# Both ends of a one-core encoder-block kernel rearranged: the last residual on TensorE, the final root on ScalarE, blocks 2 and 3 of the last down half in steps, the second v weights converted by VectorE

## The chip, the core and the metric

The kernel runs on one core of a Trainium2 chip. A core has a matrix engine (TensorE, PE in the profile; its weight loads are PEld), three engines for elementwise work (VectorE, DVE; ScalarE, ACT; GpSimd, POOL), an engine that mostly issues transfers (SyncE, SP) and 16 DMA engines. Each engine works through a queue of its own in order and waits on semaphores that others set. The metric is the device time of one execution in microseconds (us); before the change the median of three executions is 701.1 (700.32 to 701.42). The profile comes from one more execution, which took 700.69 us.

## What is computed

One layer of an encoder over 512 positions of width 1024 in float32, then a last RMSNorm:

```
h = rms_norm(x, norm_mix_g)
proj = h @ w_in                      # conv B, C, in | q | k | v | forget logits | gates
y_conv = (cb * dwconv3(cc * cin)) @ w_out_conv
y_attn = forgetting_attention(q, k, v, log_f) @ w_out_attn
x = x + (g_conv * y_conv + g_attn * y_attn) @ w_o
h = rms_norm(x, norm_ffn_g)
a, b = split(dwconv3(h @ w_up))
x = x + (silu(a) * b) @ w_down       # 2816 hidden
return rms_norm(x, norm_f_g)
```

The start of the program (the projection to v) and its end (the product with `w_down`, the residual and the last norm) are what the change touches.

## The kernel before

Everything is kept transposed: 128 features on the partitions, 512 positions in the free dimension, so x is eight blocks (m = 0 to 7) of 128 x 512. Every product is made of three matrix passes: each operand is split into a high part in the fast float32r format and a low part that holds the rest, and high x high, low x high and high x low are added in PSUM. The splitting of weights is done while TensorE works on the block before: `split` has ScalarE convert the raw block to its high part (line 244) and VectorE subtract it for the low part (line 248). The raw blocks come from memory by a stream of transfers on SyncE's queue, five buffers deep; the high and low parts have two buffers each, so the split of a block waits until TensorE has left the block before the last one.

**The start.** The first eight blocks of the stream are the v weights (v0 to v7, 128 x 520). v0 is brought in two pieces (ScalarE's queue and SyncE's) and its high part is made by VectorE; from v1 on all come by SyncE and ScalarE makes the high parts. For each block x is split too: ScalarE makes `xgh`, VectorE `xgl`. TensorE's products for block kb need `xgh` and `wh_v` first, then `wl_v`, then `xgl`.

**The product with w_down.** The 22 hidden blocks are taken in two halves (`PHASES`: 0 to 11, 12 to 21), each after its part of the up product. Most of it runs as a Strassen-like scheme, function `down`: two output blocks (2i and 2i+1), two hidden blocks (a pair q) and the two halves of the positions make a 2 x 2 x 2 product, done with seven products of 128 x 128 x 256 instead of eight (`PROD`). A step holds two such pairs; its weights are sums of weight blocks, which transfers with accumulation have built in memory long before (`group`, `tick`), and come in two pieces, `P` (three products for each pair, 768 columns) and `F` (four, 1024 columns). `STEPS` lists which (i, q) a step takes: in the last half, before the change, five steps for the blocks i = 2 and i = 0. When a pair of blocks has had its last step, `combine` adds the seven sums into x: one copy on ScalarE and six operations on VectorE (z1, a1, u3 twice, a2, a3, a4), followed by the square of each block for the last norm (`final_square`: a square and a scaling on ScalarE, an add into `ssq3` on VectorE). These follow-ups are put on a list, `later`, and emitted by `run_later` beside the splits, or at the latest by `flush`.

The blocks m = 2, 3, 6 and 7 of the last half are plain (`PLAIN`): ten hidden blocks, two halves of the positions, three passes. m = 2 and 3 come first (`pd`); m = 6 and 7 come last and in halves of the positions: the first half of both (`pdA`, bank halves), then m = 6 second half (`pdB6`) and m = 7 second half (`pdB7`).

**The end.** For each half t of the positions, `fin_sum` adds the residual (VectorE), squares and scales (ScalarE); `fin_col` adds the squares of m = 6 to `ssq3` and has TensorE sum over the partitions (`pc`); `rstd_col` makes the inverse root: VectorE forms mean + eps (`ms`), GpSimd raises it to -0.5 (`rc`). `rstd_bc` lets TensorE spread it over the partitions (`pb`); `fin_out` copies `pb` to SBUF on ScalarE (`rs`) for GpSimd's share, multiplies the eight blocks in five groups on VectorE (four) and GpSimd (one), and sends each to memory. The column sum of the first half stands after five of the ten hidden blocks of `pdB6`, its `pb` after the rest of them. Nine products without use (`warm_on`) keep TensorE at work around the last `pc`.

The order on the engines is set by a list scheduler within what `keep` fixes (all matrix products and the marked operations stay in program order).

Of the kernel before, what the change touches and what calls it, by code (L numbers as in the profile page):

```python
# [13 lines left out]
P = 128  # L14
# [34 lines left out]
    (((2, 6), (2, 7)), ((2, 8), (2, 9)), ((0, 6), (0, 7)), ((0, 8), (2, 10)), ((0, 9), (0, 10))),  # L49
# [5 lines left out]
PLAIN = [(m, k) for m in (2, 3, 6, 7) for k in range(*PHASES[1])]  # L55
PCUTS = (0, 8, 16, 20, 28, 32, 40)
# [3 lines left out]
def block_kernel(ctx, tc, xT, vecs, wv, win, wmix, wo, wup, wst, wdp, outT):  # L60
# [57 lines left out]
    groups += [list(range(n, min(n + 2, NFF))) for n in range(0, NFF, 2)]  # L118
    todo = []

    def group(i):

        ns = groups[i]
        t = dsp.tile([P, len(ns), D], F32, tag=f"sum{i}", name=f"sum{i}")
        for k, n in enumerate(ns):
            sums[n] = t[:, k, :]
        w = wst[ns[0] : ns[-1] + 1].rearrange("n p c -> p n c")
        w, f = ((lambda a, b, z=z: z[:, :, a * P : b * P]) for z in (w, t))
# [24 lines left out]
    def double(n):  # L153
        return [(f"P{n}", wst[n, :, : 6 * P], 6 * P), (f"F{n}", sums[n], D)]
# [34 lines left out]
    def load(upto):  # L189
        for k in range(len(raws), min(upto, len(stream) - 1) + 1):  # L190
            nm, src, ncol = stream[k]
            if held[0] == NRAW:
                return
            held[0] += 1
            raw = wp.tile([P, D], F32, tag="raw", name=f"raw_{nm}", bufs=NRAW)
            if k == 0:

                keep(nc.scalar.dma_start(raw[:, :VW], src[:, :VW]))
                keep(nc.sync.dma_start(raw[:, VW:ncol], src[:, VW:]))
            else:  # L200
                keep(nc.sync.dma_start(raw[:, :ncol], src))
            raws.append(raw[:, :ncol])
# [20 lines left out]
    def split(hl=None):  # L223
# [16 lines left out]
        if k == 0:  # L240
            for cs in (slice(0, VW), slice(VW, S + H)):
                keep(nc.vector.tensor_copy(hi[:, cs], raw[:, cs]))
        else:
            ins = nc.scalar.activation(hi, raw, AF.Copy)  # L244
            order["hi"] = ins.ins
            if k < KB:
                keep(ins)
# [6 lines left out]
        run_later(k, {"u": 1.7, "P": 1.6, "F": 0.75}.get(nm[0], 3.5))  # L254
# [46 lines left out]
    ex = cp.tile([P, NT], F32, tag="ex", name="ex")  # L301
    nc.gpsimd.memset(ex, -0.5)
# [5 lines left out]
    def place_of(f, s_):  # L308
        c = 2 * (f % 3 if f < 6 else 3) + s_
        return slice(c * P, (c + 1) * P)  # L310
# [19 lines left out]
    def rstd_col(sums, n, bc, name):  # L330
# [9 lines left out]
        ms = cp.tile([P, NT], F32, tag="ms", name=f"ms_{name}", bufs=2)  # L340
        nc.vector.tensor_scalar(ms[:, :n], pc[:, :n], 1.0 / D, EPS, op0=ALU.mult, op1=ALU.add)
# [742 lines left out]
    def down(ph, n0):  # L1084

        sets = ({0: X, 1: Y, 3: X, 2: Y}, {0: X, 2: Y})[ph]
        todo, wants = [], {}
        for n, d in enumerate(STEPS[ph]):
            for kind in "PF":
                prods = []  # L1090
                for s_, (i, q) in enumerate(d):
                    for f, g, b, h in PROD:
                        if (f < 3) == (kind == "P"):
                            wants.setdefault(f"{kind}{n0 + n}", []).append(("q", q))
                            prods.append((place_of(f, s_), i, place(ph, q) + g, b, h))
                todo.append((f"{kind}{n0 + n}", prods))
# [64 lines left out]
    for m, b in ((2, 4), (3, 2)):  # L1161
        flush((b,))
        p = bank(b, f"pd{m}")
        for k in kall:
            for t in range(2):
                plain(m, t, (k,), p[:, th[t]], t == 0, t == 1)
        nc.vector.tensor_add(x1[:, m, :], p, x1[:, m, :])
        later.append((0, 0.8, (), lambda m=m: final_square(m)))

    m6 = KB - 2  # L1170
    fetch(3)
    wx = fp.tile([P, 6, 2 * P], F32R, tag="gr", name="wx").rearrange("p a b -> p (a b)")
    fetch(4, [wx[:, a : a + 4 * P] for a in (80, 752)])
    fetch(5)
    flush()
    pdA, pdB6, pdB7 = bank(3, "pdA"), bank(5, "pdB6"), bank(0, "pdB7")
    pd = ((pdA[:, th[0]], pdA[:, th[1]]), (pdB6[:, th[0]], pdB7[:, th[0]]))

    def plain7(m, t, ks):
        plain(m6 + m, t, ks, pd[t][m], m == 0 or t == 1, m == 1 or t == 1)  # L1180

    def fin_sum(t, m):

        y = x1[:, m6 + m, halves[t]]
        nc.vector.tensor_add(y, pd[t][m], y)
        sq = fp.tile([P, S], F32, tag="fu", name=f"sq3_{m}{t}", bufs=3)[:, : S // 2]
        nc.scalar.activation(sq, y, AF.Square)
        nc.scalar.activation(y, y, AF.Copy, scale=col(GF + m6 + m))
        return sq

    def fin_col(t, sqs):
        s_ = ssq3[:, halves[t]]
        nc.vector.tensor_add(s_, s_, sqs[0])
        return rstd_col([s_, sqs[1]], 2, 6 + t, f"n3{t}")

    def fin_out(t, rc):
# [15 lines left out]
    warm_to = bank(2, "warm_to")[:, : 2 * P]  # L1212
# [20 lines left out]
def _layout(i):  # L1233
# [47 lines left out]
    for d in STEPS[0] + STEPS[1]:  # L1281
        wst.append(np.concatenate([wdn[2 * i + m, :, 2 * q + k] for m, k in order for i, q in d], axis=1))
# [44 lines left out]
```

## Time and profile before

| | |
|---|---|
| median of three executions | 701.1 us |
| profiled execution, whole | 700.69 us |
| its span (first to last instruction) | 698.9 us |
| busy: TensorE / VectorE / ScalarE / GpSimd | 690.2 / 498.3 / 341.8 / 156.4 us |
| bytes read / written | 112.20 / 32.51 MB |

"Busy" is the sum of an engine's instruction times; the rows of the timeline give start, duration, engine, line, operation and tiles (output <- inputs). In brackets stands how long the engine was idle before, and who ended it. In the chain of waits each row is a start and the time that the chain spends there. Two rows of the profile may overlap on one engine, since instructions are pipelined: the step from start to start is shorter than the duration.

### The profile page before, as it was taken

The page shows a single profiled execution, that of the slowest core. Times are in us where ns is not written, and L with a number is a line of the kernel's source. Part 1 is how long each engine was busy: PE and PEld are TensorE (multiplying, and loading weights), DVE is VectorE, ACT ScalarE, POOL GpSimd, SP SyncE. Part 2 cuts the span into 40 slices and gives each one's busy share as a digit, 9 for nine tenths or more (in the row PEclk, how much of TensorE's full clock was granted, in tenths as well). Part 3 has the DMA queues.
Part 4 walks back from the last instruction along what each step waited for, and adds up shares of the span by engine and source line. Part 5 has one row for each costly group of instructions (what it writes and reads, how often), then busy time and mean ns, then how long its engine had stood idle before and what let it go on. Part 6 is the DMA issues. An engine that isn't in the chain of part 4 may idle for free.

```text
span 698.9 us, 14573 instructions
## 1 busy us (share of the span) xinstructions
PE 690.2 (99%) x6005; PEld 688.1 (98%) x6005; DVE 498.3 (71%) x797; ACT 341.8 (49%) x541; POOL 156.4 (22%) x176
## 2 busy tenths in 40 slices
PE   9999999999999999999999999999999999999996
PEld 8999999999999999999999999999999999999995
DVE  6677777786687787754377777778774677877853
ACT  6665656655664433543345443455443345444542
POOL 5125645434011001035321212230000211100002
PEclk9999999999999999999999999999999999999998
DMA  8627877467379777658556637577675433224503
GB/s 308 201 74 209 200 158 200 118 163 179 92 176 268 232 212 214 225 183 207 140 133 197 170 106 199 141 171 206 191 222 177 116 118 92 84 84 133 177 1 121
DMA packets 51538, 115.31 MB, mean 165 GB/s; under 512 B 4720, under 2 KB 22256, under 8 KB 51472
## 3 DMA queue, kind: packets, MB, share of 16 engines
q1 hardware_dynamic: 36880, 93.73, 41.4%
q0 software_dynamic: 13328, 19.44, 17.5%
q10 hardware_dynamic: 1264, 1.22, 0.5%
q8 instruction: 47, 0.77, 0.4%
q14 instruction: 19, 0.16, 0.1%
HBM read 112.20 MB, written 32.51 MB: 207 GB/s over the span
## 4 chain that ended last, share of the span: by engine, by line
PE 92%; DVE 2%; ACT 2%; issue 1%; DMA 1%; ACTq 0%; SPq 0%; POOL 0%; DVEq 0%
PE p_up L277 26%; PE p_in L277 14%; PE dn L295 12%; PE p_up L295 8%; PE gs L295 8%; PE p_wo L277 6%; PE yc L295 3%; PE ya L277 3%; PE pd L277 2%; PE o L659 2%; PE pa L478 2%; PE pb L480 1%; PE tp L644 1%; PE pdB L277 1%; PE pdA L277 1%
## 5 line engine op out<-in xcount | busy, mean ns | idle before, releaser
L277 PE MATMUL p_up<-x1h,wh_up 128*128 128x256 f32 x536 | 104.5, 276 | 0.0
L277 PE MATMUL p_up<-x1l,wh_up 128*128 128x256 f32 x536 | 104.4, 276 | 0.0
L277 PE MATMUL p_up<-x1h,wl_up 128*128 128x256 f32 x536 | 104.3, 276 | 0.0
L244 ACT ACTIVATE wh_up<-raw_up 128x1024 fp32r<-128x1024 f32 x44 | 46.7, 1061 | 89.2 <-PE p_up L277 75.7
L277 PEld LDWEIGHTS p_up<-x1h,wh_up 128*128 128x128 f32 x536 | 80.8, 188 | 0.0
L277 PEld LDWEIGHTS p_up<-x1l,wh_up 128*128 128x128 f32 x536 | 80.7, 188 | 0.0
L277 PEld LDWEIGHTS p_up<-x1h,wl_up 128*128 128x128 f32 x536 | 80.6, 188 | 0.0
L134 POOL DMA_DIRECT2D sum<-in_wst_dram x45 | 47.1, 1122 | 116.4 <-DMA sum<-sum 88.8
L248 DVE TENSOR_TENSOR wl_up<-raw_up,wh_up 128x1024 fp32r<-128x1024 f32 x44 | 53.8, 1223 | 20.8 <-ACT wh_up L244 20.8
L244 ACT ACTIVATE wh_F<-raw_F 128x1024 fp32r<-128x1024 f32 x29 | 30.8, 1063 | 54.6 <-PE ya L277 25.9
L277 PE MATMUL p_in<-xgh,wh_in 128*128 128x256 f32 x288 | 56.8, 279 | 0.0
L277 PE MATMUL p_in<-xgh,wl_in 128*128 128x256 f32 x288 | 56.6, 278 | 0.1
L277 PE MATMUL p_in<-xgl,wh_in 128*128 128x256 f32 x288 | 56.5, 277 | 0.0
L976 DVE TENSOR_TENSOR fz<-p_up,rb_n 128x512 f32<-128x512 f32 x44 | 30.3, 690 | 31.3 <-PE p_up L277 31.3
L248 DVE TENSOR_TENSOR wl_F<-raw_F,wh_F 128x1024 fp32r<-128x1024 f32 x29 | 35.5, 1223 | 17.5 <-ACT wh_F L244 17.5
L277 PEld LDWEIGHTS p_in<-xgh,wh_in 128*128 128x128 f32 x288 | 44.7, 188 | 0.7
L989 POOL TENSOR_TENSOR ge<-fu,fu 128x512 f32<-128x512 f32 x11 | 17.1, 1551 | 120.3 <-DVE fu L573 107.5
L277 PEld LDWEIGHTS p_in<-xgh,wl_in 128*128 128x128 f32 x288 | 43.6, 188 | 0.3 <-DVE wl_in L248 0.3
L277 PEld LDWEIGHTS p_in<-xgl,wh_in 128*128 128x128 f32 x288 | 43.6, 188 | 0.0
L295 PE MATMUL p_up<-x1h,wh_up 128*128 128x256 f32 x168 | 40.3, 277 | 0.0
L295 PE MATMUL p_up<-x1l,wh_up 128*128 128x256 f32 x168 | 40.2, 276 | 0.0
L244 ACT ACTIVATE wh_P<-raw_P 128x768 fp32r<-128x768 f32 x29 | 24.4, 842 | 26.1 <-PE dn L295 14.1
(307 smaller groups left out, 2044.5 us busy)
## 6 DMA issues: line engine op xcount, KB each, us to landing
raw_up<-in_wup_dram SPq DMA_DIRECT2D x44, 512.0 KB, 4.3
raw_F<-sum SPq DMA_DIRECT2D x29, 512.0 KB, 4.6
raw_in<-in_win_dram SPq DMA_DIRECT2D x24, 512.0 KB, 4.5
raw_P<-in_wst_dram SPq DMA_DIRECT2D x29, 384.0 KB, 3.5
sum<-in_wst_dram POOLq DMA_DIRECT2D x29, 256.0 KB, 5.6
sum<-in_wst_dram SPq DMA_DIRECT2D x14, 512.0 KB, 5.6
sum<-in_wst_dram POOLq DMA_DIRECT2D x14, 512.0 KB, 7.3
sum<-sum SPq DMA_DIRECT2D x28, 256.0 KB, 5.9
```

Of the source, the lines that this page charges most:

```text
L134: return lambda: keep(nc.gpsimd.dma_start(dst, src, accum_op=ALU.add))
L244: ins = nc.scalar.activation(hi, raw, AF.Copy)
L248: ins = nc.vector.tensor_sub(lo, raw, hi.bitcast(F32))
L277: keep(nc.tensor.matmul(out[:, cs], w, x[:, cs], start=start and i == 0 and c == 0, stop=stop and i == 2 and c == len(cut) - 1,))
L295: keep(nc.tensor.matmul(out, wl if x == 1 else wh, xl if x == 2 else xh, start=opens and bk not in seen, stop=closes and bk not in left,))
L478: keep(nc.tensor.matmul(pa[t][:, :VW], xt, w[:, :VW], start=start, stop=stop))
L480: keep(nc.tensor.matmul(pb[t], xt, w[:, VW:], start=start and t % 2 == 0, stop=stop and t % 2 == 1))
L644: keep(nc.tensor.transpose(tp[:, ks], pt[:, ks], ident))
L659: keep(nc.tensor.matmul(o[:, os_], vv[:, kb, pr, e, :], x[:, kb, cs], start=e == 0 and kb == 0 and i == 0, stop=e == 1 and kb == nk - 1 an ...
L976: nc.vector.tensor_mul(z, p, rb2)
L989: keep(nc.gpsimd.tensor_mul(ge, a.rearrange(halves_of, h=2), b.rearrange(halves_of, h=2)))
```

## The change

- The blocks 2 and 3 of the last down half (i = 1) are no longer plain but take steps: (1,6)/(1,7), (1,8)/(1,9) and a last step with the single pair (1,10). A step with one pair has half the columns; its group of sums stands alone. In step 15 the two pairs change places. `PLAIN` holds m = 6 and 7 only.
- The second half of the residual of m = 7 is split into high and low parts and added by TensorE, as two products with the identity into `pdB7`; the last square and scaling read PSUM directly.
- For the two final column sums, ScalarE takes the root of mean + eps (Sqrt) and VectorE the reciprocal, instead of VectorE and GpSimd's power.
- In `fin_out`, the first group's multiplication comes ahead of ScalarE's copy of `pb`.
- The second v block comes on ScalarE's queue, and VectorE makes its high part.
- Splits of the `dp` blocks carry no follow-up work with them (`"d": 0`).

```
-    (((2, 6), (2, 7)), ((2, 8), (2, 9)), ((0, 6), (0, 7)), ((0, 8), (2, 10)), ((0, 9), (0, 10))),
+    (
+        ((2, 6), (2, 7)), ((2, 8), (2, 9)), ((0, 6), (0, 7)), ((2, 10), (0, 8)), ((0, 9), (0, 10)),
+        ((1, 6), (1, 7)), ((1, 8), (1, 9)), ((1, 10),),
+    ),
-PLAIN = [(m, k) for m in (2, 3, 6, 7) for k in range(*PHASES[1])]
-PCUTS = (0, 8, 16, 20, 28, 32, 40)
+PLAIN = [(m, k) for m in (6, 7) for k in range(*PHASES[1])]
+PCUTS = (0, 4, 12, 20)
...
-                keep(nc.sync.dma_start(raw[:, :ncol], src))
+                keep((nc.scalar if k == 1 else nc.sync).dma_start(raw[:, :ncol], src))
...
-        if k == 0:
-            for cs in (slice(0, VW), slice(VW, S + H)):
+        if k < 2:
+            for cs in (slice(0, VW), slice(VW, S + H)) if k == 0 else (slice(0, S + H),):
                 keep(nc.vector.tensor_copy(hi[:, cs], raw[:, cs]))
...
-        run_later(k, {"u": 1.7, "P": 1.6, "F": 0.75}.get(nm[0], 3.5))
+        run_later(k, {"u": 1.7, "P": 1.6, "F": 0.75, "d": 0}.get(nm[0], 3.5))
...
+        if n == 2:
+            nc.scalar.activation(ms[:, :n], pc[:, :n], AF.Sqrt, bias=eps, scale=1.0 / D)
+            rc = cp.tile([P, NT], F32, tag="rc", name=f"rc_{name}", bufs=2)
+            nc.vector.reciprocal(rc[:, :n], ms[:, :n])
+            return rc
...
-    for m, b in ((2, 4), (3, 2)):
...
+    idr = gh[:, 40, :P]
+    nc.scalar.activation(idr, ident, AF.Copy)
+    xlast = (gh[:, 41, :], gl[:, 41, :])
+    y7 = x1[:, KB - 1, halves[1]]
+    nc.scalar.activation(xlast[0], y7, AF.Copy)
+    nc.vector.tensor_sub(xlast[1], y7, xlast[0].bitcast(F32))
...
+        if m + t == 2:
+            for i, x in enumerate(xlast):
+                keep(nc.tensor.matmul(pd[t][m], idr, x, start=i == 0, stop=False))
...
-        nc.vector.tensor_add(y, pd[t][m], y)
+        r = y
+        if m + t == 2:
+            r = pd[t][m]
+        else:
+            nc.vector.tensor_add(y, pd[t][m], y)
...
-        nc.scalar.activation(rs, pb, AF.Copy)
...
-            eng.tensor_mul(y, y, r.unsqueeze(1).to_broadcast([P, b - a, S // 2]))
+            keep(eng.tensor_mul(y, y, r.unsqueeze(1).to_broadcast([P, b - a, S // 2])))
+            if g == 0:
+                keep(nc.scalar.activation(rs, pb, AF.Copy))
```

The queues show what stands where. First VectorE's, from the low part of the last but one weight block on. Before (`wl_dp` low parts of weights, `x1` the residual, `pd2`/`pd3` the plain sums of m = 2 and 3, `cz10`/`cu10` the intermediate sums of block 0, `sq3_` squares; `ssq3` their sum):

```order
L248 TENSOR_TENSOR wl_dp2_8559<-raw_dp2_8369,wh_dp2_8558 128x512
L1057 TENSOR_TENSOR x1_4014<-x1_4014,cz10_8500 128x512
L1167 TENSOR_TENSOR x1_4014<-pd2_8430,x1_4014 128x512
L1061 TENSOR_TENSOR x1_4014<-x1_4014,cu10_8504 128x512
L1077 TENSOR_TENSOR ssq3_4522<-ssq3_4522,sq3_0_8564 128x512
L1077 TENSOR_TENSOR ssq3_4522<-ssq3_4522,sq3_1_8568 128x512
L248 TENSOR_TENSOR wl_dp3_8598<-raw_dp3_8397,wh_dp3_8597 128x1024
L1077 TENSOR_TENSOR ssq3_4522<-ssq3_4522,sq3_2_8601 128x512
L1167 TENSOR_TENSOR x1_4014<-pd3_8521,x1_4014 128x512
L248 TENSOR_TENSOR wl_dp5_8613<-raw_dp5_8490,wh_dp5_8612 128x1024
L1077 TENSOR_TENSOR ssq3_4522<-ssq3_4522,sq3_3_8605 128x512
```

And now (`dn11...` are the banks of block 1, `cz11`/`cu11` its intermediate sums):

```order
L254 TENSOR_TENSOR wl_dp2_8613<-raw_dp2_8569,wh_dp2_8612 128x1024
L1070 TENSOR_TENSOR x1_4017<-x1_4017,cz10_8542 128x512
L1074 TENSOR_TENSOR x1_4017<-x1_4017,cu10_8576 128x512
L1059 TENSOR_TENSOR x1_4017<-dn112_8453,x1_4017 128x512
L1090 TENSOR_TENSOR ssq3_4525<-ssq3_4525,sq3_0_8618 128x512
L1056 TENSOR_TENSOR cz11_8626<-dn114_8455,cz11_8626 128x256
L1090 TENSOR_TENSOR ssq3_4525<-ssq3_4525,sq3_1_8622 128x512
L1063 TENSOR_TENSOR cu11_8630<-dn115_8456,cz11_8626 128x256
L1064 TENSOR_TENSOR x1_4017<-dn113_8454,x1_4017 128x256
L1067 TENSOR_TENSOR x1_4017<-x1_4017,dn113_8454 128x512
L1070 TENSOR_TENSOR x1_4017<-x1_4017,cz11_8626 128x512
L1074 TENSOR_TENSOR x1_4017<-x1_4017,cu11_8630 128x512
```

The two adds of the plain sums are gone, the six operations of block 1 stand behind the last weights and block 0's last two, and the adds of squares lie between them. The second place follows directly, VectorE's queue around the first half's end; before:

```order
L1185 TENSOR_TENSOR x1_4014<-pdA_8616,x1_4014 128x256 x2
L1193 TENSOR_TENSOR ssq3_4522<-ssq3_4522,sq3_00_8681 128x256
L341 TENSOR_SCALAR ms_n30_8709<-pc_n30_8704 128x2
L1185 TENSOR_TENSOR x1_4014<-pdB6_8617,x1_4014 128x256
L1204 TENSOR_TENSOR x1_4014<-x1_4014,pb_n30_8728 128x256
L1204 TENSOR_TENSOR x1_4014<-x1_4014,pb_n30_8728 128x2x256 x2
L1204 TENSOR_TENSOR x1_4014<-x1_4014,pb_n30_8728 128x256
```

And now:

```order
L1203 TENSOR_TENSOR x1_4017<-pdA_8644,x1_4017 128x256
L1090 TENSOR_TENSOR ssq3_4525<-ssq3_4525,sq3_2_8636 128x512
L1203 TENSOR_TENSOR x1_4017<-pdA_8644,x1_4017 128x256
L1090 TENSOR_TENSOR ssq3_4525<-ssq3_4525,sq3_3_8640 128x512
L1211 TENSOR_TENSOR ssq3_4525<-ssq3_4525,sq3_00_8712 128x256
L1203 TENSOR_TENSOR x1_4017<-pdB6_8645,x1_4017 128x256
L352 RECIPROCAL rc_n30_8742<-ms_n30_8740 128x2
```

Two more adds of squares lie between the sums of `pdA`; the sum of `pdB6` has moved ahead of the reciprocal that stands for `ms`. The third place is the start of ScalarE's queue, before:

```order
L98 ACTIVATE tbl<-ones 32x1
L198 DMA raw_v_129<-in_wv_dram 128x264
L455 ACTIVATE xgh<-x_127 128x256
L455 ACTIVATE xgh<-xs_132,x_127 128x256
L455 ACTIVATE xgh<-xs_132,x_127 128x512
L244 ACTIVATE wh_v_187<-raw_v_135 128x520
L442 ACTIVATE ssq_120<-x_127 128x256
```

And now:

```order
L101 ACTIVATE tbl<-ones 32x1
L204 DMA raw_v_132<-in_wv_dram 128x264
L207 DMA raw_v_138<-in_wv_dram 128x520
L468 ACTIVATE xgh<-x_130 128x256
L468 ACTIVATE xgh<-xs_135,x_130 128x256
L468 ACTIVATE xgh<-xs_135,x_130 128x512
L455 ACTIVATE ssq_123<-x_130 128x256
L455 ACTIVATE ssq_123<-xs_135 128x256
```

The transfer of the second v block (`raw_v_138`, 128 x 520) has come in, on this queue, and its conversion (`wh_v_187` before) has left it for VectorE's.

More of the change, by code (lines that the diff above doesn't have):

```diff
@@ L117, in block_kernel @@
     ngate = len(groups)
-    groups += [list(range(n, min(n + 2, NFF))) for n in range(0, NFF, 2)]
+    groups += [list(range(n, min(n + 2, NFF - 1))) for n in range(0, NFF - 1, 2)] + [[NFF - 1]]
+    nstep = [len(d) for d in STEPS[0] + STEPS[1]] + [2] * (2 * (KB - GS))
     todo = []
@@ L153, in double @@
     def double(n):
-        return [(f"P{n}", wst[n, :, : 6 * P], 6 * P), (f"F{n}", sums[n], D)]
+        h = nstep[n]
+        return [(f"P{n}", wst[n, :, : 3 * h * P], 3 * h * P), (f"F{n}", sums[n][:, : 4 * h * P], 4 * h * P)]
     def gate_n(j):
```

46 lines of the change are left out of this document (22 added, 24 removed).

## The prediction

> **What bounds the kernel now.** I read the page's busy table first, then the chain of work that ended last in order of time, then the timeline of single engines around both ends.
>
> ```profile
> PE 690.2 (99%) x6005; PEld 688.1 (98%) x6005; DVE 498.3 (71%) x797; ACT 341.8 (49%) x541; POOL 156.4 (22%) x176
> L277 PE MATMUL p_up<-x1h,wh_up 128*128 128x256 f32 x536 | 104.5, 276 | 0.0
> ```
>
> TensorE is busy for 690.2 of 698.9 us, so 8.7 us are all that waiting can give back; beyond that only fewer products help. A product lasts 0.276 us, but the next one starts well before that, as the chain shows:
>
> ```profile
> 2.12 4.52 DMA xs<-in_xT_dram
> 6.66 0.72 ACT xgh L455
> 7.38 0.60 ACT wh_v L244
> ...
> 636.59 23.80 PE dn L295 x210
> 660.39 13.60 PE pd L277 x120
> 673.99 6.80 PE pdA L277 x60
> 680.79 1.70 PE pdB L277 x15
> 682.49 0.84 PE pc_n L336 x8
> 683.33 1.86 PE pdB L277 x15
> 685.19 0.44 PE pb_n L350 x4
> 685.64 3.46 PE pdB L277 x30
> ...
> 689.12 0.44 DVE x L1185
> ...
> 689.58 0.42 ACT sq L1187
> ...
> 690.04 0.62 PE pc_n L336 x4
> ...
> 690.69 0.17 DVE ms_n L341
> ...
> 690.93 0.71 POOL rc_n L343
> ...
> 691.68 0.72 PE pb_n L350 x4
> ```
>
> The 120 `pd` products take 13.60 us: one step is 0.1133 us. From 636.59 to 689.10 TensorE runs without a gap; a product less there is 0.1133 us less. Behind 689.10 a chain of small steps follows through five engines, 3.30 us up to the end of `pb` at 692.40. At the start the second v block waits for its x (landed at 6.64), for the x's high part and then for that of its weights; its first product comes at 8.03 (row further down).
>
> **The change part by part.** The sum is made against the profiled execution, 700.69 us (span 698.9 and 1.79 around it). The median of the three runs is 701.1, 0.41 above it.
>
> *Products.* Blocks m 2 and 3 took 2 x 10 x 2 x 3 = 120 plain products; five Strassen-like steps of 7 x 3 make 105. Fifteen less are 15 x 0.1133 = -1.70 us. The residual of the last block is two products more, +0.23 us. Splitting the new weights lies beside these products, and so do the two small conversions for the identity and the residual, which stand in the up stage between weight conversions. Six more accumulating transfers (17 groups of three instead of 15) run beside the up stage, where 45 of them made no wait of TensorE; cost nothing, and if SyncE's queue should hold a weight load back, that load's delay.
>
> *The wait that the new place of block 1 makes.* Before, 13.6 us of plain products lay between the last step and `pdA`, and VectorE combined block 0 behind them. Now block 1 ends in the last step, and only `pdA` and five pairs of `pdB`, 6.80 + 1.70 = 8.50 us, lie between it and the column sums `pc`, which need the squares of all blocks. Behind the last step stand, in the order of VectorE's queue, the low parts of two weight blocks, two operations of block 0, six of block 1, four adds of squares, two sums of `pdA` and the add of the half. Their steps:
>
> ```profile
> 661.66 1.22 DVE L248 TENSOR_TENSOR wl_dp<-raw_dp,wh_dp 128x1024 fp32r<-128x1024 f32 x1
> 662.80 0.69 DVE L1077 TENSOR_TENSOR ssq<-ssq,sq 128x512 f32<-128x512 f32 x1
> 663.40 0.68 DVE L1046 TENSOR_TENSOR x<-dn,x 128x512 f32<-128x512 f32 x1
> ...
> 664.86 0.41 DVE L1050 TENSOR_TENSOR cu<-dn,cz 128x256 f32<-128x256 f32 x1
> 665.19 0.68 DVE L1054 TENSOR_TENSOR x<-x,dn 128x512 f32<-128x512 f32 x1
> ...
> 660.58 1.05 ACT L244 ACTIVATE wh_dp<-raw_dp 128x1024 fp32r<-128x1024 f32 x1
> ...
> 668.52 0.72 ACT L1078 ACTIVATE x<-x,vec 128x512 f32<-128x512 f32 x1
> 669.15 0.62 ACT L1076 ACTIVATE sq<-x 128x512 f32<-128x512 f32 x1
> ```
>
> From start to start an operation over 1024 columns takes 1.14 us, over 512 columns 0.60, over 256 columns 0.33; a ScalarE operation over 512 columns 0.63 when the next waits for it. Call T the first product of `pdA`. The high part of the last weight block takes the buffer that the last F weights leave after their eighth of twelve products, at about T-0.25; it ends at T+0.81, and its low part runs on VectorE from T+0.85 to T+1.99. Four operations of 0.60 (`cz` and `cu` into block 0, block 1's first sum, the add of square 0) lead to T+4.39, `cz` of block 1 to T+4.72. Square 1 comes from ScalarE behind a scaling at T+4.80; its add leads to T+5.40, two short ones to T+6.06, three long ones to T+7.86, a sum of `pdA`, the add of square 2, the other sum and the add of square 3 to T+9.72. ScalarE gets block 1's second half at T+7.95, squares it, scales two halves and only then, at T+9.78, squares the half that the column sum waits for: done at T+10.20, added at T+10.65, `pc` at T+10.70. TensorE is there at T+8.50 and waits **2.20 us**; behind `pc` in its queue stand all remaining products. Bounds: 1.70 if ScalarE's scalings don't count, 2.60 if the last weights come free only at T and 0.15 later.
>
> *Reciprocal behind the sum of `pdB6`.* Before, `ms` stood ahead of that sum on VectorE and POOL's power followed; `pb` came without a wait. Now the order is the sum of `pdB6`, then the reciprocal, and the sum waits for the end of the very products that stand ahead of `pb`.
>
> ```profile
> 38.96 1.28 ACT L697 ACT_TABLE_LOAD   x1
> 40.26 0.63 ACT L697 ACTIVATE fe<-fe 32x512 f32<-32x512 f32 x1
> ...
> 42.20 0.20 ACT L698 ACTIVATE tbl<-fe 32x1 f32<-32x1 f32 x1
> L627 DVE RECIPROCAL m<-m x32: 147/154/168, 57.8 to 167.1; 128x1 f32<-128x1 f32 x32
> 690.51 0.96 PE L1210 MATMUL warm_to<-gl,gh 128*128 128x256 f32 x6
> ```
>
> The sum starts 0.04 after the products' end, the reciprocal 0.34 later, takes 0.15, and `pb` follows 0.05 behind: 0.58 after the end, where a product following at its normal step starts 0.16 ahead of that end (0.276 - 0.113). That is **+0.74 us**. The table load (1.28 us) and the root (two columns; nearest the 0.20 of the one-column activation) end 2.1 us behind `pc`'s start, ahead of the sum's 2.9, so they are covered. In the trace the activation starts 0.02 us after the table load ends. [...]
>
> *The last chain.* The add in front of the last square goes: 0.46 us with its gap. `ms` and POOL's power, 0.17 + 0.71 and gaps of 0.14, become a root of 0.20 (the nearest row; at most the 0.42 of a square over 256 columns, at least nothing) and a reciprocal of 0.15. By this chain `pb` would start 1.62 us after the last product, but the six keep-warm products behind `pc` hold TensorE: their row starts 0.47 behind `pc`'s start, and the sixth step is over 1.29 behind it, so `pb` starts at 0.50 + 1.29 = 1.79 and ends at 2.51 instead of 3.30: **-0.79 us** (between -0.7 and -0.95). VectorE's first multiplication and ScalarE's copy of the root only change places, so the later ones and the transfers start as before.
>
> *The start.*
>
> ```profile
> 1.03 0.44 ACTq L198 DMA_DIRECT2D raw_v<-in_wv_dram  x1
> 2.59 0.43 SPq L201 DMA_DIRECT2D raw_v<-in_wv_dram  x1
> 3.50 0.99 DVE L242 CAST wh_v<-raw_v 128x264 fp32r<-128x264 f32 x2 [2.51 <-DMA raw_v<-in_wv_dram]
> 5.54 0.48 DVE L468 SCALAR_TENSOR_TENSOR xgl<-xs,x,xgh 128x256 fp32r<-128x256 f32 x1
> 9.16 0.64 ACT L244 ACTIVATE wh_v<-raw_v 128x520 fp32r<-128x520 f32 x1 [0.57 <-DMA raw_v<-in_wv_dram]
> 9.71 0.71 ACT L455 ACTIVATE xgh<-xs,x 128x512 fp32r<-128x512 f32 x1
> 8.03 0.39 PE L478 MATMUL pa<-wh_v,xgh 128*128 128x264 f32 x1 [0.56 <-ACT wh_v L244]
> 8.00:11.00 3.00, 2.97 (x24) 2.97 (x25) 2.53 (x4) 2.36 (x5) 1.89 (x4) 1.00 1.06 398
> ```
>
> ScalarE's 0.60 us for the second weights leaves the path: VectorE is free at 6.02 and casts them by about 7.0 (at most 0.99 us), ahead of x's high part at 7.38. That would start TensorE at 7.43 instead of 8.03. But its 24 products take 2.97 us, and the third block's x is ready at 10.42 if its transfer (waited for at 9.16) comes no earlier: then 0.15 us are given back. I take **-0.45 us**. The weights' transfer moves from SyncE's 2.59 to ScalarE's queue at about 1.5, ahead of the x that the chain waits for; if it pushes that x back by the 0.6 us saved, the gain is nothing. If all comes earlier it is 0.72 at most: TensorE was idle for 0.56, and 0.16 are the last product running out.
>
> *Sum:* -1.70 + 0.23 + 2.20 + 0.74 - 0.79 - 0.45 = **+0.23 us**: 700.92 against the profiled execution, 701.33 against the median; I say 701.1, between them. With every bound on the good side (1.70, -0.95, -0.72) it is -0.70, on the bad side (2.60, -0.70, 0) +1.17.
>
> **The rivals.** *The ends shorten as they read* (nothing waits at `pc`): VectorE's queue would have to be over at T+8.45 instead of T+10.65, with five operations fewer than the order shows, or each a fifth shorter. Then 700.69 - 2.0 = 698.7, and 698.0 if `pb` doesn't wait either. For it speaks that TensorE waited nowhere in this stage before; against it the fixed order and the sum of steps.
>
> *The clock falls in the new wait* (slower). It decides if TensorE's idle time at `pc` is long enough to lose the granted clock; the longest idle time that this trace has between 1 and 690 us is 0.56 us ahead of 8.03, and the window behind it shows a clock of 1.00, so longer ones are untested. At worst all 47 products behind `pc` take twice 0.1133: +5.3 us, 706; over half of them +2.7 us, 703.6. [...]
>
> *The change doesn't shorten the start*: the transfers only swap order, and 0.45 us are missing: 701.4 to 701.8. It stays within the forecast's range.
>
> **How the numbers follow.** No measurement of this kernel tells less than about 0.2%, 1.4 us, from no change. The forecast with its bounds (699.7 to 702.5 around 701.1, the runs' own spread taken in) gets 0.70, the short ends 0.14, the clock 0.08, and a wait longer than the bound (the last weight block landing late, one for one) 0.08. Faster by over 0.2% are the short ends and a little of the forecast, 0.16; slower are the clock and the longer wait, 0.15; within, 0.69. The range 699.5 to 702.8 leaves out the short ends and most of the clock.
>
> **What would show it.** A wait of 1.7 to 2.6 us of `pc` ahead of 15 `pdB` products, released by the add of a square on VectorE; a wait of 0.6 to 1.0 us of the first `pb`, released by the reciprocal; 315 `dn` products and no `pd`; 2.4 to 2.6 us from the last `pdB` to the end of the last `pb`; the second v block's first product at 7.3 to 8.0. I am wrong if `pc` doesn't wait, if steps behind it are longer than 0.12 us, or if TensorE waits inside `dn`.

## The result and the profile after

| | before | after |
|---|---|---|
| median of six executions | 701.14 us (700.32 to 701.42) | 704.82 us (702.75 to 707.89) |
| profiled execution, whole | 700.69 us | 702.75 us, the shortest of the six |
| its span / mean granted clock | 698.9 us / 0.996 | 701.0 us / 0.997 |
| mean granted clock of all six | | 0.997, 0.995, 0.994, 0.991, 0.991, 0.989 |

The ratio is 1.0056, with a 95% interval of 1.0035 to 1.0078: slower by more than 0.2%, and outside the range that was forecast. Two things are to be explained: 2.06 us between the two profiled executions, and another 1.3 to 5.1 us by which the other executions of the changed kernel exceed the profiled one, at lower mean clocks. The kernel before shows no such spread.

TensorE's waits from the last down half to the last column sum, before and then after (engine, line, tile, releaser: total, times, longest):

```profile
PE pc_n L336 <- ACT sq L1187: 0.3, 1, 0.3
PE pb_n L350 <- POOL rc_n L343: 0.2, 1, 0.2
```

```profile
PE pc_n L344 <- DVE ssq L1211: 2.1, 1, 2.1
PE pb_n L363 <- DVE rc_n L352: 0.6, 1, 0.6
```

In the view of before, both rows belong to the last column sum and its `pb` (at 690.04 and 691.68 us); the first half's `pc` and `pb` did not wait. Their rows in the timeline of TensorE, before and then after (start, duration; in brackets the idle time and who ended it):

```profile
682.33 0.56 PE L336 MATMUL pc_n<-ones,ssq 128*128 128x1 f32 x4
685.03 0.60 PE L350 MATMUL pb_n<-ident,rc_n 128*128 128x128 f32 x4
```

```profile
683.43 0.58 PE L344 MATMUL pc_n<-ones,ssq 128*128 128x1 f32 x4 [2.06 <-DVE ssq L1211]
686.86 0.71 PE L363 MATMUL pb_n<-ident,rc_n 128*128 128x128 f32 x4 [0.59 <-DVE rc_n L352]
```

Both forecast waits are there. The chain of waits of the changed kernel shows where they stand (start, time on the chain):

```profile
637.16 35.26 PE dn L301 x311
...
672.45 1.07 ACT wh_dp L250
673.54 1.23 DVE wl_dp L254
...
681.29 1.22 ACT x L1091 x2
...
682.85 0.44 DVE ssq L1211
683.29 0.14 issue
683.43 1.02 PE pc_n L344 x8
684.45 1.83 PE pdB L283 x15
...
686.86 0.71 PE pb_n L363 x4
687.57 0.23 PE pdB L1193 x2
687.80 3.42 PE pdB L283 x30
...
692.36 0.81 PE warm_to L1229 x6
693.18 0.46 PE pb_n L363 x4
```

From 672.45 the chain leaves TensorE for eleven microseconds and runs through the last weights, block 1's sums, the squares and the scalings, as the forecast had it. In place of the 2.20 us that the forecast's queue gave, TensorE is idle for 2.06. At the start the chain differs. First the rows of the timeline of before, then of after (start, duration, engine, line, operation; in brackets the idle time and who ended it):

```profile
4.23 0.51 ACT L455 ACTIVATE xgh<-xs,x 128x256 fp32r<-128x256 f32 x1 [0.75 <-DMA xs<-in_xT_dram]
4.88 0.41 PE L478 MATMUL pa<-wh_v,xgh 128*128 128x264 f32 x2
```

```profile
5.16 0.51 ACT L468 ACTIVATE xgh<-xs,x 128x256 fp32r<-128x256 f32 x1 [1.72 <-DMA xs<-in_xT_dram]
5.72 0.81 PE L491 MATMUL pa<-wh_v,xgh 128*128 128x264 f32 x2 [0.33 <-ACT xgh L468]
8.77 0.28 PE L491 MATMUL pa<-wh_v,xgh 128*128 128x264 f32 x1
```

The second half of the first x block is there 0.93 us later, TensorE waits for it, and the second v block's first product comes at 8.77 where the kernel before had 8.03. At the start of `dn`, 0.57 us of this are left (637.16 against 636.59).

Last, the end, before and after:

```profile
692.49 0.38 ACT L1200 ACTIVATE rs<-pb_n 128x256 f32<-128x256 f32 x1 [1.95 <-PE pb_n L350]
692.95 1.27 POOL L1204 TENSOR_TENSOR x<-x,rs 128x512 f32<-128x512 f32 x1 [1.32 <-ACT rs L1200]
693.35 1.86 SPq L1205 DMA_DIRECT2D out_dram<-x  x3
```

```profile
693.66 0.42 DVE L1221 TENSOR_TENSOR x<-x,pb_n 128x256 f32<-128x256 f32 x1 [0.80 <-PE pb_n L363]
694.11 2.77 SPq L1224 DMA_DIRECT2D out_dram<-x  x3
694.18 0.38 ACT L1223 ACTIVATE rs<-pb_n 128x256 f32<-128x256 f32 x1 [1.51 <-DVE x L1221]
694.64 1.27 POOL L1221 TENSOR_TENSOR x<-x,rs 128x512 f32<-128x512 f32 x1 [4.81 <-ACT rs L1223]
```

Counted from the end of the last `pb` (692.40 and 693.64), ScalarE's copy starts at 0.54 in place of 0.09 and GpSimd's product at 1.00 in place of 0.55; SyncE's last issue, which is queued behind the wait for GpSimd, ends at 3.24 in place of 2.81. The whole stretch from `pb` to the end of the span takes 7.36 us in place of 6.50.

### The profile page after: what moved, and what is told of

Same layout as the page of the kernel before. It is cut to its first block, busy times and chain, and to the rows that moved or that the text cites. A ratio compares the mean times of both kernels' runs of the same rounds, so it can differ in the third digit from the quotient of the medians.

```text
span 701.0 us, 14597 instructions
## 1 busy us (share of the span) xinstructions
PE 689.5 (98%) x5992; PEld 687.3 (98%) x5992; DVE 503.8 (72%) x806; ACT 345.3 (49%) x549; POOL 160.9 (23%) x181
## 4 chain that ended last, share of the span: by engine, by line
PE 93%; DVE 2%; ACT 2%; issue 1%; DMA 0%; ACTq 0%; SPq 0%; DVEq 0%
PE p_up L283 26%; PE p_in L283 14%; PE dn L301 13%; PE gs L301 8%; PE p_up L301 8%; PE p_wo L283 6%; PE yc L301 3%; PE ya L283 3%; PE pa L491 2%; PE pb L493 2%; PE p_g L283 2%; PE o L672 2%; PE tp L657 1%; PE s L628 1%; PE pdB L283 1%; PE s L629 1%
## 5 line engine op out<-in xcount | busy, mean ns | idle before, releaser
L139 POOL DMA_DIRECT2D sum<-in_wst_dram x51 | 52.8, 1119 | 125.4 <-DMA sum<-sum 88.0
L250 ACT ACTIVATE wh_F<-raw_F 128x1024 fp32r<-128x1024 f32 (+1 forms) x32 | 33.6, 1049 | 58.2 <-PE ya L283 25.9
L254 DVE TENSOR_TENSOR wl_F<-raw_F,wh_F 128x1024 fp32r<-128x1024 f32 (+1 forms) x32 | 38.6, 1207 | 20.0 <-ACT wh_F L250 19.8
L250 ACT ACTIVATE wh_P<-raw_P 128x768 fp32r<-128x768 f32 (+1 forms) x32 | 26.7, 833 | 28.5 <-PE dn L301 16.2
```

Source lines behind the costliest of these rows:

```text
L254: ins = nc.vector.tensor_sub(lo, raw, hi.bitcast(F32))
```

## Experiments

The kernel before ran beside every group: 700.80 us for e1 to e4, 700.89 for e5 to e8, 700.86 for e9 to e12, 700.95 for e13 and e14. Intervals are of the ratio to it.

### e1: the changed kernel again

No edit.

> The changed kernel once more, unedited, so that a profile of an ordinary execution of it exists: the profiled one (702.75 us, span 701.0, clock 0.997) was the shortest of six, and the others were up to 5 us longer at mean clocks down to 0.989. Every theory expects 704 to 705.5 us for the median, about 3 to 4 above the kernel before, and executions spread over 3 to 5 us where those of the kernel before spread over about 1. If this profile falls on a longer execution, its granted clock by stretches says where the rest goes. Theory 'head': below full clock in the first 15 us. Theory 'late wait': below full clock between 683 and 695 us, behind the wait of 2.1 us for the last addition of the squares. Theory 'steps': below full clock somewhere in the last down half, 640 to 683 us.

Measured: 705.93 us (704.48 to 709.37), ratio 1.0077 [1.0059, 1.0095]. This time the profile fell on an execution at a mean clock of 0.989, span 705.4. The table by stretches of e1 (stretch, length; busy time and count of PE, PEld, DVE, ACT, POOL; granted clock, DMA share, GB/s):

```profile
680.00:684.00 4.00, 1.93 (x16) 1.77 (x14) 2.86 (x6) 3.98 (x9) 0.00 (x0) 0.93 0.00 0
684.00:688.00 4.00, 4.00 (x20) 4.00 (x20) 0.00 (x0) 1.43 (x2) 0.00 (x0) 0.50 0.00 0
688.00:692.00 4.00, 3.41 (x16) 3.12 (x16) 1.66 (x5) 1.13 (x3) 0.70 (x1) 0.50 0.08 26
692.00:694.00 2.00, 2.00 (x13) 2.00 (x12) 1.21 (x3) 0.07 (x1) 0.59 (x1) 0.58 0.63 219
```

In the four microseconds from 684 TensorE starts 20 operations where the shortest execution of the same program has 30 in 3.41 busy us. The clock falls to 0.50 at about 683.5, right behind the wait, and comes back at about 693.7. From `pc` to the last product it takes 12.27 us and not 7.79: 4.5 us more, all of the 4.4 us between the two spans. Theory "late wait" holds; the head and the steps show 1.00.

### e2, e3: the head undone, and the head alone

e2 is the changed kernel without these lines, e3 the kernel before with them:

```
+                keep((nc.scalar if k == 1 else nc.sync).dma_start(raw[:, :ncol], src))
+        if k < 2:
+            for cs in (slice(0, VW), slice(VW, S + H)) if k == 0 else (slice(0, S + H),):
```

> The changed kernel with the head of the kernel before: the second v weights go back to SyncE's queue and to ScalarE for their high part. The profile of the changed kernel has the second half of xs0 0.9 us later, and its second block's first product 0.74 us later, of which 0.57 is left at the start of the last down half. Theory 'head costs only its delay': 0.5 to 0.75 us less than the changed kernel, 704.1 for the median, executions spread as before over 3 to 5 us. Theory 'head also costs the clock': 702 to 702.5 us and a spread of about 1 us. Theory 'head gains, and the difference at 637 us has another origin' (what I forecast): 0.45 us more than the changed kernel, 705.3.

> The kernel before with the changed head alone. Theory 'head costs only its delay': 0.5 to 0.75 us slower than the kernel before, 701.7 to 701.9, spread about 1 us. Theory 'head also costs the clock': 703 to 704.5 us, with a spread of 3 to 5 us and mean clocks down to 0.99. Forecast theory: 700.65, 0.45 us faster.

Measured: e2 704.93 us (702.23 to 706.65), 1.0045 [1.0030, 1.0060], mean clocks 0.990 to 0.997; `dn` starts at 636.59 as before. e3 701.39 us (701.09 to 703.11), 1.0015 [1.0007, 1.0024], clocks at 0.994 and above. So the head doesn't cost the late clock; it costs 0.59 us in the median, where I had forecast a gain of 0.45. But e3 has two groups, six executions from 701.1 to 701.4 and five from 702.2 to 703.1, which no theory had. Its profile is of the upper group; from the timeline of TensorE in e3:

```profile
4.64 0.69 PE L480 MATMUL pb<-wh_v,xgh 128*128 128x256 f32 x2
6.23 0.81 PE L478 MATMUL pa<-wh_v,xgh 128*128 128x264 f32 x2 [0.90 <-ACT xgh L455]
...
8.99 0.64 PE L478 MATMUL pa<-wh_v,xgl 128*128 128x264 f32 x2
9.44 0.50 PE L480 MATMUL pb<-wh_v,xgl 128*128 128x256 f32 x2
9.77 0.40 PE L478 MATMUL pa<-wh_v,xgl 128*128 128x264 f32 x2
```

A pair of products lasts 0.64 us up to 9.4 and 0.40 from then on; in the kernel before the quick pace is reached at 4.9. The gap of 0.90 us falls into the slow time, and the slow pace lasts 3.2 us beyond it. `dn` starts at 638.64, 2.05 us late. The row of the granted clock says 1.00 throughout, but the trace's record of the clock begins only where full clock is first granted: at 9.65 us in e3 and at 4.18 us in the kernel before, close to where the products become quick. What lies ahead counts as 1.00 only because nothing is recorded there.

### e4: ScalarE's copy first again

```
+        keep(nc.scalar.activation(rs, pb, AF.Copy))
         for g, (a, b) in enumerate(((0, 1), (1, 3), (6, 8), (3, 5), (5, 6))):
...
-            if g == 0:
-                keep(nc.scalar.activation(rs, pb, AF.Copy))
```

> The changed kernel with one exchange undone: ScalarE's copy of the broadcast column (rs) stands ahead of VectorE's first product again. Theory 'exchange costs': rs begins 0.45 us earlier behind the last broadcast product, GpSimd's share, SyncE's issue for it and the one behind it with it, and the stretch behind the broadcast is 6.5 us again as in the kernel before in place of 7.36: 0.4 to 0.9 us less than the changed kernel. Theory 'exchange is even' (what I forecast): within 0.15 us of the changed kernel, the stretch still 7.2 to 7.4.

Measured: 704.61 us (703.79 to 707.49), 1.0058 [1.0043, 1.0072], against 705.93 for e1 beside it; the clock's spread blurs the difference. The trace is clearer: from `pb` to the end 6.89 us (696.71 to 703.6) in place of 7.36. The exchange costs, 0.47 us here, but 0.39 of the 0.86 remain.

### e5, e12: the wait filled, wholly and by half

```
     plain7(0, 1, kall[:5])
+    warm_on(18)
     rcA = fin_col(0, sqA)
```

e12 has `warm_on(9)`.

> The changed kernel with 18 products whose results nobody reads (the same that keep TensorE busy behind the last group) put into the wait of 2.06 us ahead of the additions of the squares of half A: 18 x 0.113 = 2.03 us. The wait stays, TensorE is only no longer idle in it. Theory 'the idle wait costs the clock': the granted clock stays at 1.00 to the last product in every execution, the mean clock is 0.996 to 0.997, and the time falls to that of the executions of the changed kernel that lose no clock, 702.2 to 703.0 us, with what is left of the spread (1 to 2 us) from the head. Rival 'the clock falls for the work itself' (a denser last down half): no change, 704.5 to 706 us, clock 0.50 in a stretch of 3 to 10 us as before.

> e5 with 9 products in the late wait in place of 18: TensorE is idle there for about 1.05 us and not for 2.06. Theory 'any idle stretch can cost the clock by where it falls': fewer executions than in the changed kernel with a stretch at 0.50, median 703 to 704.5 us. Theory 'an idle stretch of about 1 us is too short': clock 1.00 throughout, median 702.3 to 703.0 us (e5's 702.04 and 0.7 for the broadcast's wait, which VectorE's order brings back here).

Measured: e5 702.04 us (701.70 to 704.66), 1.0024 [1.0013, 1.0034]; e12 704.04 us (702.70 to 705.98), 1.0048 [1.0034, 1.0063]. The additions start when they did (683.39), so the wait is the same; TensorE is only busy in it. From the timeline of e5, and then its table by stretches:

```profile
681.15 2.32 PE L1229 MATMUL warm_to<-gl,gh 128*128 128x256 f32 x18
683.39 0.58 PE L344 MATMUL pc_n<-ones,ssq 128*128 128x1 f32 x4
```

```profile
680.00:684.00 4.00, 4.00 (x36) 3.91 (x34) 2.88 (x6) 3.97 (x9) 0.00 (x0) 1.00 0.00 0
684.00:688.00 4.00, 4.00 (x36) 4.00 (x36) 1.39 (x4) 2.22 (x5) 0.33 (x1) 1.00 0.02 4
```

Doing useless work in the wait makes the kernel faster by 2.8 to 3.9 us in the median (704.82 and 705.93 against 702.04). 0.7 to 0.8 of that is another effect: in this kernel the scheduler put the reciprocal ahead of the sum of `pdB6`, and `pb` no longer waits (from the start of `pc` to the start of `pb` 2.72 us in place of 3.43, and to the product behind `pb` 3.08 in place of 3.90). That measures the forecast's 0.74 as 0.71 to 0.82. The rest is the clock. One of seven executions still has a mean clock of 0.994, and it isn't settled why. With half of the wait filled, TensorE is idle for 1.00 us, as e12's timeline shows:

```profile
683.80 0.58 PE L344 MATMUL pc_n<-ones,ssq 128*128 128x1 f32 x4 [1.00 <-DVE ssq L1211]
```

Two of six executions have clocks of 0.992 and 0.995 (705.62 and 705.98 us), four have 0.997 or more. No profile shows where those two lost it; by these few executions a shorter idle time makes the loss rarer, and 1 us is not known to be safe.

### e6: no steps

Blocks 2 and 3 plain again, with the old `STEPS`, `PLAIN`, `PCUTS` and banks, and with follow-up work beside the splits of the `dp` blocks as before.

> The changed kernel with blocks 2 and 3 of the last down half put back to ten plain blocks of the kernel before; the head, the last residual through TensorE, the root on ScalarE and the exchange at the end stay. Theory 'the steps make the wait, and the wait the clock': no wait of 2 us ahead of the additions of half A, clock 1.00 throughout; kernel before + head 0.6 + residual 0.23 + wait for the broadcast 0.74 - last chain 0.88 + exchange 0.45 = 701.9 us (701.6 to 702.4), spread from the head alone. Rival 'the other edits cost the clock': 704 us or more, with a stretch at 0.50.

Measured: 701.13 us (700.66 to 703.26), 1.0011 [1.0002, 1.0019]. No wait at `pc`, clock 1.00 in every window behind 680. It is 0.8 below the expectation, because the wait for the broadcast (0.74 of the sum) isn't there: again the reciprocal stands ahead of the sum of `pdB6`. So the wait at `pc` and the lost clock come with the steps. The second wait hangs on the order that the scheduler picks for these two operations: it is there with the steps in the changed kernel and in e12, and not in e5, which has the steps too.

### e7, e14: the conversion alone, and the queue alone

e7 is the changed kernel with `nc.sync.dma_start` for the second v weights again; e14 is the kernel before with only

```
-                keep(nc.sync.dma_start(raw[:, :ncol], src))
+                keep((nc.scalar if k == 1 else nc.sync).dma_start(raw[:, :ncol], src))
```

> The changed kernel with the transfer of the second v weights back on SyncE's queue, in its old place, and their high part still made by VectorE. Theory 'the queue costs, the conversion does not': the second half of xs0 lands as in the kernel before (ScalarE reads it at 4.2 us and not at 5.2 to 5.8), TensorE has no gap ahead of 7 us, and the last down half starts at 636.6 or earlier, 0.5 to 2 us ahead of the changed kernel's; the median falls by 0.6 to 1 us (the stretch at 0.50 behind the late wait stays and blurs it). Rival 'the conversion costs': the start is as late as in the changed kernel.

> The kernel before with one thing changed: the transfer of the second v weights on ScalarE's queue (their high part stays with ScalarE). Theory 'the queue costs': the second half of xs0 is read at 5.2 us or later, not at 4.2, TensorE waits 0.3 to 1.3 us for it, the last down half starts 0.4 to 0.6 us later or 2 us later, the median is 701.2 to 701.5 with executions at 702.2 to 703.1 as in e3 (701.39). Rival 'VectorE's conversion costs' (e7's start was 0.53 late with the transfer in its old place): 700.7 to 701.0, one group.

Measured: e14 701.52 us (701.12 to 704.13), 1.0018 [1.0008, 1.0029], six executions from 701.1 to 701.5 and five from 703.0 to 704.1: the move of the transfer to another queue alone has the whole price of the head and both groups. e7 704.49 us (704.31 to 707.11), 1.0066 [1.0052, 1.0080], too blurred by the late clock to be read by its time. In its trace the second half of xs0 is read at 4.26 as in the kernel before, but `dn` starts at 637.12, no earlier than in the changed kernel. From its timeline:

```profile
8.62 0.36 PE L491 MATMUL pa<-wh_v,xgh 128*128 128x264 f32 x1 [1.01 <-DVE wh_v L248]
```

TensorE waits 1.01 us for VectorE's cast, and the cast for the weights, which landed at 7.77 by the chain of waits (issued at 2.59, 5.18 us). So in neither place did the conversion by VectorE start TensorE earlier than the 8.03 of the kernel before; that it would gain with its transfer early and x in time was not shown.

### e13: the gap at the start filled

e3, and where TensorE waits for the second half of xs0:

```
+                    for _ in range(4 if i == 0 and t0 else 0):
+                        keep(nc.tensor.matmul(warm[:, :P], ones, ones, start=True, stop=True))
```

> e3 (the kernel before with the changed head alone) with four unread products of 128 columns put where TensorE waits for the second half of xs0; they take 0.4 us at the quick pace of the products and 0.85 at the slow one. Theory 'the idle gap lengthens the slow pace': the second group of e3's executions (5 of 11 between 702.2 and 703.1 us) is gone, every execution stands between 701.0 and 702.0, and pairs of products last 0.64 us to no later than 7.5 us. Rival 'the second group is late transfers': as many executions above 702.1 us as in e3, and the wait for xs0 in them longer than 1 us.

Measured: 701.48 us (700.92 to 701.93), 1.0008 [0.9999, 1.0016]. The upper group is gone, with x landing as late as in e3's upper group (ScalarE reads it at 5.95, there at 5.67). From the timeline of TensorE in e13:

```profile
5.18 1.91 PE L490 MATMUL warm<-ones 128*128 128x128 f32 x8
6.75 0.72 PE L478 MATMUL pa<-wh_v,xgh 128*128 128x264 f32 x2
7.31 0.40 PE L480 MATMUL pb<-wh_v,xgh 128*128 128x256 f32 x2
```

The four unread products show as eight instructions and take 1.91 us, more than the 0.85 expected, so the second half of x is taken up about 0.25 us after it is ready (its high part is done at 6.46). The pace is quick from 7.3 and not from 9.5, and the record of the clock has its first full grant at 7.27. So the transfer's delay makes the lower group (0.3 to 0.6 us in e3), and the idle gap, where it falls into the slow time, the upper one.

### e8: the squares of half A asked for later

The order at the end (the edits inside `fin_col`, `rstd_col` and `plain7` are left out here):

```
-    plain7(0, 1, kall[:5])
-    rcA = fin_col(0, sqA)
-    plain7(0, 1, kall[5:])
-    fin_out(0, rcA)
-    sqB = [fin_sum(1, 0)]
-    plain7(1, 1, kall)
+    plain7(0, 1, kall)
+    fin_add(0, sqA)
+    sqB = []
+    rcA = fin_col(0, sqA, lambda: sqB.append(fin_sum(1, 0)))
+    plain7(1, 1, kall[:6])
+    fin_add(1, sqB)
+    fin_out(0, rcA)
+    plain7(1, 1, kall[6:])
```

`fin_add` is the add of the square that `fin_col` had; the function given to `fin_col` runs between the additions and the root.

> The changed kernel with the additions of the squares of half A put behind all 30 products of pdB6 (in place of 15), the sum of pdB6 ahead of its root, and the broadcast of half A behind 20 of pdB7's 32 products (in place of ahead of them). TensorE waits 0.4 to 0.5 us and not 2.06 for the squares, and nothing for the broadcast. Theory 'the long idle wait is what costs': the clock stays at 1.00, the last product ends at 689.0 us and not 691.2 (from the shortest profile of the changed kernel), the median is 700.4 to 701.2 us, 4 to 5 less than the changed kernel. Rival 'any wait there costs the clock': 702.5 us or more, with a stretch at 0.50.

Measured: 700.93 us (700.56 to 702.82), 1.0005 [0.9996, 1.0013]: 3.9 to 5.0 us below the changed kernel. The idle time at `pc` is 0.37 us, which is 1.7 less; the wait at the first `pb` (0.8) is gone as well; the clock stays, and the rest of the gain fits that. From the timeline of e8, and from its table by stretches:

```profile
683.36 0.58 PE L344 MATMUL pc_n<-ones,ssq 128*128 128x1 f32 x4 [0.37 <-DVE ssq L1213]
```

```profile
684.00:688.00 4.00, 4.00 (x36) 4.00 (x36) 1.01 (x3) 2.50 (x5) 0.00 (x0) 1.00 0.02 4
```

### e9, e10, e11: what can be kept

e9 is e8 with the old head and ScalarE's copy first. e10 is the kernel before with the residual through TensorE and the root on ScalarE alone. e11 is e6 with ScalarE's copy first.

> The kernel with the late additions of half A (e8: 700.93 us, its profile 700.63), and the two edits undone that cost: the head as in the kernel before (e3: 0.59 for it alone) and ScalarE's copy ahead of VectorE's first product at the end (0.47 by the stretch behind the broadcast, 7.36 against 6.89). Theory 'the costs add': 700.93 - 0.6 - 0.45 = 699.9 us (699.6 to 700.2), 0.1 to 0.2% under the kernel before, spread of about 1 us with no execution in a second group 1.6 us up. Rival 'the tail is set by the outgoing transfers of half A': the exchange gives nothing once the last product ends 2 us earlier, 700.3 to 700.5.

> The kernel before with only the last residual through TensorE and the root on ScalarE (no steps, old head, ScalarE's copy first). Terms from the profiles: last chain -0.88, products of the residual +0.23, broadcast of half A with no wait 0. Theory 'only the last chain gains': 700.85 - 0.65 = 700.2 us (699.9 to 700.5), spread of about 1 us. Rival 'the tail gives it back' (in every kernel with the root on ScalarE the stretch from the last issue to the end of the span was 4.1 us, against 3.7 before): 700.6 to 700.9.

> e6 (no steps, changed head, exchange) with the exchange undone, so that its price is read where no clock falls. Theory 'exchange costs': the stretch from the last broadcast product to the end of the span goes from 7.36 or so to 6.9, the median from 701.13 to 700.7 us. Rival 'even': 701.0 to 701.3. Executions fall in two groups 1.6 us apart, as in e3 and e6, since the head is the changed one; between this and e10 only the head differs, 0.4 to 0.6 us in the median.

Measured: e9 **699.56 us** (699.29 to 700.23), 0.9982 [0.9973, 0.9990]; e10 700.18 (699.88 to 701.58), 0.9992 [0.9983, 1.0000]; e11 700.80 (700.51 to 702.41), 1.0004 [0.9996, 1.0013]. e9 is faster than both kernels, ends just below the range of 'the costs add', and has no second group; e10 is where 'only the last chain gains' put it, and e11 is 0.1 above its expectation. Between e11 and e10 lies the head, 0.62 us; between e6 and e11 the exchange, 0.33 by the medians and 0.31 by the stretch behind `pb` (6.81 and 6.50). From the chain of waits of e9:

```profile
682.70 1.02 PE pc_n L344 x8
683.73 0.34 PE pdB L1195 x2
684.07 2.05 PE pdB L283 x18
686.12 0.46 PE pb_n L365 x4
```

`pc`, products and `pb` follow each other without a wait but the 0.37 ahead of `pc`.

## Why the prediction was wrong

| term | forecast | measured |
|---|---|---|
| fifteen products less | -1.70 | -1.69 (`dn` to the wait: 44.21 and 45.90) |
| two residual products | +0.23 | +0.19 (32 products in 3.65, 30 in 3.46) |
| wait at `pc` | +2.20 | +2.06 |
| `pc` itself | 0 | +0.18 (1.02 and 0.84) |
| wait of the first `pb` | +0.74 | +0.82 (end of `pc` to end of `pb`: 3.12 and 2.30) |
| last chain | -0.79 | -0.88 (2.42 and 3.30) |
| start | -0.45 | +0.57 |
| from `pb` to the end | 0 | +0.86 |
| **span, profiled execution** | **+0.23** | **+2.1** |
| median above the profiled execution: the clock, and in part the start | not in the sum | +2.1 |

**What held.** The products, both waits with their places and releasers, and the last chain: each within 0.15 us. The rival that the ends shorten as they read is refuted by the 2.06 us at `pc`.

**The step that cost most: the clock as a rival of 0.08.** The forecast had the mechanism, its place and its price (up to 5.3 us; e1 lost 4.5), but it left the clock out of the sum and gave it little weight, although the longest idle time in the trace of before was 0.56 us and so told nothing of 2 us. That a wait of 2.2 us would keep the clock, as the weight of 0.08 supposed, was shown by no run. What is measured here: 2.06 us of idle time were enough in 27 of the 30 executions of the five runs with that wait (changed kernel, e1, e2, e4, e7; mean clock 0.995 or less), while 84 of the 88 of e3, e6, e8 to e11, e13 and e14 show 0.996 or more. (The mean is below 1.00 in every execution, since the clock also falls behind the last product, at 693.68 us in the kernel before and 696.45 in the changed one; one of the four exceptions, in e8 at 0.995, is among its fastest.) In e1 the products behind the wait step by 0.23 us (15 in 3.42 us by its chain of waits), past the 0.12 that the forecast had named as a sign of being wrong. The profile on which the terms could be checked was one of the three that escaped, and that was luck. With the clock's case at its measured weight, the forecast would have been 702.5 to 705.4 us (700.92 and the 1.6 to 4.5 us that e7 and e1 took longer from `pc` to the last product: 9.40 and 12.27 against 7.79).

**The start** had the wrong sign. That "if it pushes that x back by the 0.6 us saved, the gain is nothing" was taken as the bad bound, as though the x of the second block were the only one at stake. The x that was pushed back is the second half of the first block's, which TensorE needs next (e14); and the bound left out what an idle gap there does to the pace (e3, e13). Measured +0.6 in the median and about +2 in some executions.

**The exchange at the end** was costed at nothing by "the later ones and the transfers start as before". That is true for VectorE alone (its last product ends 2.57 us behind `pb`, before 2.45). ScalarE's copy is what GpSimd's share waits for, and SyncE's last two transfers wait behind that share: 0.3 to 0.5 us (e4, e11). The other 0.4 us lie behind the last issue: 4.1 us to the end of the span in all kernels with steps (the changed one, e1, e2, e4, e5, e7, e8, e9, e12), 3.6 to 3.7 in all without (before, e3, e6, e10, e11, e13, e14). It isn't the root on ScalarE, as e10's expectation had it: e6, e10 and e11 have that root and not the 4.1. Why the steps do it wasn't found.

## What to carry to other kernels

A wait of TensorE can have two prices, its length and the clock of the products behind it; here, with 47 products behind a wait of 2.06 us, the second was 1.6 us in e7 and 4.5 in e1. Put such a request later, or, where it can't move, fill the wait with products that nobody reads, and judge by several executions, since the one that is profiled may have escaped. When a transfer changes its queue, list every transfer that it now runs beside, and which of them is needed first; and when two readers of one tile change places, look for who waits for the second one on other engines.

## What was not expected of the hardware

The stretches at clock 0.50 come in two lengths: 3.41 us in e4 (685.51 to 688.92) and e7 (684.11 to 687.52), 10.24 us in e1 (683.46 to 693.70) and e2 (683.35 to 693.59), three times as long (from the granted clock of half-microsecond stretches). The fall comes 0.1 to 0.7 us after the idle time has ended. The traces' own record of the clock says more. From the first full grant to the fall it has 689.49 us in the kernel before (4.18 to 693.68) and in the changed one (6.96 to 696.45), and 679.25 in e1 and e7. That is 202 and 199 times 3.413 us: each of these lengths is a whole multiple of the single stretch of e4 and e7. Where points counted on in such steps lie differs between executions: the first full grants of these two kernels are 2.78 us apart.

That also fits which profile escaped. In the four that fell, the whole wait of 2.06 us lies between two neighbouring points. In the changed kernel's first profile the points, counted on from the first full grant at 6.96, have one at 682.80, which divides the wait into 1.43 and 0.63 us. In e12's profile 1.00 us of idle time cost no clock (1.00 in every stretch from 680 to 692 us). The three lengths are those of single profiles, and no run moves the points on purpose. Why the clock came back after one stretch or after three isn't shown either; in e1 and e2 the first of the three begins with 1.7 and 0.9 us of the thin `pc` products and the second holds the wait for `pb`, while in e4 and e7 the single stretch has 0.6 and 0.5 us of `pc` and ends before that wait.

At the start the same record gives the first full clock at 4.18 us in the kernel before, 6.96 in the changed one, 9.65 in e3, 9.73 in e14 and 7.27 in e13. In e3 and e14 the point one step earlier (6.24 and 6.32) falls at the end of an idle gap of 0.90 and 1.00 us, and the clock stayed low there; the changed kernel's gap of 0.33 us ahead of 6.96 did no such harm. That fits the two groups of executions: in these two profiles the gap stood ahead of the first full grant, and full clock came one stretch of 3.41 us later. In e1, with its first full grant at 4.21 (683.46 less 679.25), a gap of 1.23 us ahead of 6.31 left the pace quick: the next pairs last 0.51 and 0.40 us, in e3 0.81 and 0.63.

The root's table load took 1.28 us (from 683.94 in the changed kernel) and the root began 0.02 us later, as in the trace of before.
